# A two-layer trunk on one core: two norm rows carried through a DRAM row, and five turns of compressed weights moved next to the value products

## The chip, the cores and the metric

The kernel runs on one core of one Trainium2 chip. The metric is the device time of one execution in microseconds (us). The core has five engines that each work through an instruction list of their own: PE (TensorE, the matrix engine), DVE (VectorE), ACT (ScalarE), POOL (GpSimd) and SP (SyncE, which here only issues transfers). They wait for each other on semaphores. Transfers are issued by an engine onto a DMA queue and done by 16 DMA engines.

## What is computed

A sequence of 512 positions of width 1024 goes through two layers. Layer 0 mixes by gated linear attention, layer 1 by a sparse attention with a compressed, a selected and a windowed branch, whose keys and values come from a shared projection of the input of layer 1. Both layers also attend to a memory of 256 rows, and both end in a gated convolutional FFN. Cut to what the change touches:

```python
def rmsnorm(x, g):
    y = x * lax.rsqrt(jnp.mean(x * x, axis=-1, keepdims=True) + EPS)
    return y * g

mem_kv = rmsnorm(mem, norm_mem[i]) @ w_mem_kv[i]             # both layers: 256 rows, 1024 -> 512
kv = (rmsnorm(h, kv_norm) @ w_kv).reshape(B, S, 6, G, Dh)    # layer 1: 512 rows
kc, vc = compress(kv[0], 0), compress(kv[1], 1)              # 31 blocks of 32 positions, stride 16
...
s_c = einsum('bgrqd,bgkd->bgrqk', qb, kc) + common_bias(d_c)   # 12 heads x 512 queries x 31 blocks
p_c = masked_softmax(s_c, d_c >= 0)
o_c = einsum('bgrqk,bgkd->bgrqd', p_c, vc)
o = gb[..., 0:1] * o_c + gb[..., 1:2] * o_s + gb[..., 2:3] * o_w
```

All is float32.

## The kernel before

Activations lie transposed: a tile `h[k]` holds 128 of the 1024 features on its partitions and the 512 positions along the free axis. A float32 product is made of three faster ones: each operand is split into a rounded part and the rest (`xh`, `xl` for activations, `wh`, `wl` for weights, written by ACT and DVE at L287/L288 or L304/L305), and PE adds `xh*wh + xh*wl + xl*wh`. A projection onto 128 outputs (`projA`, L326) is 24 such matmuls, called steps 0 to 23, into one bank of PSUM. PSUM's banks come in four names, `acc`, `sc`, `pt` and `po`, with two banks each, and a bank is used again when its readers have finished. The weights come through SP's queue into `wraw`.

A normalised projection needs one factor for each position. The squares are summed over the feature tiles into `sqacc`, and `rms_sums` sums over the partitions by eight narrow matmuls (L368); DVE scales (`rc`, L378) and POOL takes the power -1/2 (L379). `rc` then holds position 128t+p at partition p, column t. Where the outputs stand on partitions and the positions along the free axis, the factor is wanted as a row, the same on all partitions (`rb`). `rms_rows` makes it on PE: it transposes each column of `rc`, broadcast to 128 columns, into `pt` (L386), and ACT copies the bank out (L390).

Each engine's order is fixed when the kernel is built: a scheduler lists the instructions as the program issues them, by estimated ready times, and `behind` adds order where the author wants it. The `at` argument of `projA` runs code at a given step of a projection.

Three places matter.

- First memory (`mem_kv` with l = 0, at about 40 to 60 us): `rms_sums` at step 12 of the first key projection; `rms_rows` after the sixth group of three products of the value projection; then the keys are scaled by the row (`mkf`, DVE), split (`mK`, ACT L412 and DVE), and the values scaled by `rcm` (`mV`, ACT). The same function runs again for layer 1.
- Second mixer (`nsa_layer`, at about 580 to 603 us): four projections `kvc` (j = 0, 1 and m = 0, 1) into the two banks of `acc`. In the second one the sums come at step 0 and the rows at step 12 (`rms_at`). Each result is then scaled by the row (`kf`, DVE L1576), which frees its bank, and stored four times into `T` by SP's queue. The third projection takes the bank of the first.
- Sparse attention (`nsa_layer`, at about 700 to 822 us): twelve steps s; a pair of heads a has an even step (query tiles 0 and 3) and an odd one (1 and 2), and each step goes through places i = 0 to 5. A step computes the scores of step s+1 (`sc`, `po` from `K` and `Qh`, `Ql`), softmax weights on DVE, ACT and POOL, brings them by DMA into `R`, turns them on PE (`pt<-ident,R`, L1718, and the copies into `PT`, L1913), runs at i = 4 the value products of step s-1 (`po<-PT,V`: 20 matmuls of 64 columns, of which the profile makes 40; `values`), and fills in matmuls of other projections (L1717 with `xh`, `wh`, and L1003 in the last steps). The compressed branch is the generator `compressed(a)` in three pieces: products with the compressed keys and the exponentials; the sums and the scaling of `Pc` on POOL (L1825, L1826); and the turn: four transposes `pt<-ident,Pc` of 64 columns on PE, a copy to `PcT` by ACT (L1831) and a subtraction by DVE (L1832). For a pair a+1 the first piece runs at i = 4 of an odd step, the second at i = 0 of the next, even step, and the third at i = 0 of the odd step after it. `PcT` is first read at i = 4 of that odd step, by `values`.

## Time and profile before

| | |
|---|---|
| time, median of 3 runs | 1223.89 us (1223.47 to 1224.72) |
| the profiled execution's own time | 1224.9 us |
| its span | 1223.1 us, granted TensorE clock 0.998 |
| PE, weight loads | 1211.6 us (99%), 1077.9 us (88%) |
| DVE, ACT, POOL | 912.5 us (75%), 729.7 us (60%), 275.2 us (23%) |
| DMA queues, share of 16 engines | hardware 34.0%, POOL's 10.7% |

The profile is one execution. Busy times are the sums over an engine's instructions, with overlapping matmuls not counted twice; the span is from the first instruction to the last. The time lies 1.8 us above the span. In the groups of instructions the three numbers after a colon are the least, the median and the longest duration in ns. Durations of matmuls include the time in the pipeline, so that one starts before the one ahead has ended; what a matmul costs is read from the distance of the starts.

### The profile page before, as it was taken

The page shows a single profiled execution, that of the slowest core. Times are in us where ns is not written, and L with a number is a line of the kernel's source. Part 1 is how long each engine was busy: PE and PEld are TensorE (multiplying, and loading weights), DVE is VectorE, ACT ScalarE, POOL GpSimd, SP SyncE. Part 2 cuts the span into 40 slices and gives each one's busy share as a digit, 9 for nine tenths or more (in the row PEclk, how much of TensorE's full clock was granted, in tenths as well). Part 3 has the DMA queues.
Part 4 walks back from the last instruction along what each step waited for, and adds up shares of the span by engine and source line. Part 5 has one row for each costly group of instructions (what it writes and reads, how often), then busy time and mean ns, then how long its engine had stood idle before and what let it go on. Part 6 is the DMA issues. An engine that isn't in the chain of part 4 may idle for free.

```text
span 1223.1 us, 22059 instructions
## 1 busy us (share of the span) xinstructions
PE 1211.6 (99%) x8321; PEld 1077.9 (88%) x8321; DVE 912.5 (75%) x1637; ACT 729.7 (60%) x1459; POOL 275.2 (23%) x290
## 2 busy tenths in 40 slices
PE   9999999999999999999999999999999999999997
PEld 8887889889999998888888878878899999998887
DVE  7667886698888889644776878875788888889431
ACT  7656655467666667333544677764576666675331
POOL 1000000014444420000003366660034444400000
PEclk9999999999999999999999999999999999999999
DMA  7541113236666652323725467643256666633221
GB/s 262 155 138 60 36 36 104 103 101 171 158 157 156 156 128 86 125 87 109 210 104 172 125 207 234 206 166 121 72 144 163 157 156 156 156 104 108 103 69 69
DMA packets 59776, 163.09 MB, mean 133 GB/s; under 512 B 7309, under 2 KB 13384, under 8 KB 59670
## 3 DMA queue, kind: packets, MB, share of 16 engines
q1 hardware_dynamic: 47638, 140.66, 34.0%
q0 software_dynamic: 10944, 19.93, 10.7%
q8 instruction: 65, 1.06, 0.4%
q10 hardware_dynamic: 1088, 1.10, 0.3%
q14 instruction: 41, 0.34, 0.1%
HBM read 116.13 MB, written 2.15 MB: 97 GB/s over the span
## 4 chain that ended last, share of the span: by engine, by line
PE 94%; DVE 2%; issue 1%; ACT 1%; DMA 1%; POOL 1%; POOLq 0%; DVEq 0%; ACTq 0%
PE pt L1186 18%; PE acc L326 10%; PE po L1186 9%; PE acc L1419 7%; PE acc L1003 6%; PE po L1358 5%; PE sc L1358 5%; PE sc L1186 5%; PE po L346 3%; PE acc L789 3%; PE po L1717 3%; PE acc L1717 2%; PE acc L1482 2%; PE acc L1623 2%; PE acc L346 2%; PE sc L1717 1%
## 5 line engine op out<-in xcount | busy, mean ns | idle before, releaser
L287 ACT ACTIVATE wh<-wraw 128x1024 fp32r<-128x1024 f32 (+1 forms) x105 | 109.4, 1043 | 140.6 <-PE sc L1358 29.6
L288 DVE TENSOR_TENSOR wl<-wraw,wh 128x1024 fp32r<-128x1024 f32 (+1 forms) x105 | 128.7, 1227 | 74.8 <-ACT wh L287 74.0
L1175 DVE TENSOR_TENSOR wl<-wraw,wh 128x1024 fp32r<-128x1024 f32 x76 | 72.6, 955 | 7.0 <-ACT wh L1172 7.0
L326 PE MATMUL acc<-xh,wh 128*128 128x512 f32 x184 | 72.6, 395 | 0.0
L326 PE MATMUL acc<-xl,wh 128*128 128x512 f32 x184 | 71.9, 391 | 0.0
L326 PE MATMUL acc<-xh,wl 128*128 128x512 f32 x184 | 71.9, 391 | 0.0
L1419 PE MATMUL acc<-a,wh 128*128 128x512 f32 x228 | 71.1, 389 | 0.0
L1166 POOL DMA_DIRECT2D wraw<-rbw x38 | 33.4, 879 | 153.3 <-DVE wl L1175 113.9
L1175 DVE TENSOR_TENSOR wl<-rbw,wh 128x1024 fp32r<-128x1024 f32 x38 | 46.5, 1225 | 26.5 <-ACT wh L1172 26.5
L1056 DVE SCALAR_TENSOR_TENSOR hc<-acc,ntap,hc 128x511 f32<-128x511 f32 x76 | 56.9, 749 | 10.0 <-ACT hc L1053 8.0
L1172 ACT ACTIVATE wh<-wraw 128x1024 fp32r<-128x1024 f32 x76 | 63.9, 843 | 0.6 <-DMA wraw<-rbw 0.5
L1797 POOL TENSOR_TENSOR P<-P,ssm 128x256 f32<-128x256 f32 (+3 forms) x48 | 61.8, 1309 | 1.9
L1056 DVE SCALAR_TENSOR_TENSOR hc<-acc,vec,hc 128x511 f32<-128x511 f32 x76 | 56.9, 749 | 3.0 <-ACT hc L1053 1.7
L1789 ACT ACTIVATE P<-P,smn 128x128 f32<-128x128 f32 (+3 forms) x96 | 53.3, 558 | 7.5 <-DVE smn L1787 6.9
L1161 POOL TENSOR_TENSOR rbw<-s,rbw 128x512 f32<-128x512 f32 x36 | 47.8, 1329 | 36.8 <-DVE xh L1064 19.0
L1358 PE MATMUL po<-a,wh 128*128 128x512 f32 x144 | 56.0, 389 | 0.0
L1358 PE MATMUL sc<-a,wh 128*128 128x512 f32 x144 | 56.0, 389 | 0.0
L1172 ACT ACTIVATE wh<-rbw 128x1024 fp32r<-128x1024 f32 x38 | 40.2, 1059 | 23.4 <-issue 20.5
L1419 PEld LDWEIGHTS acc<-a,wh 128*128 128x128 f32 x228 | 42.8, 188 | 8.9
L1155 POOL TENSOR_TENSOR s<-wraw,rbw 128x512 f32<-128x512 f32 x34 | 44.8, 1317 | 21.4 <-DVE wl L1175 21.4
L1172 ACT ACTIVATE wh<-s 128x512 fp32r<-128x512 f32 x38 | 24.0, 632 | 42.1 <-PE pt L1186 42.1
L1419 PE MATMUL acc<-a,wl 128*128 128x512 f32 x114 | 44.3, 389 | 0.0
(726 smaller groups left out, 4338.7 us busy)
## 6 DMA issues: line engine op xcount, KB each, us to landing
wraw<-in_wp SPq DMA_DIRECT2D x156, 512.0 KB, 3.2
rbw<-in_wp SPq DMA_DIRECT2D x38, 512.0 KB, 4.4
rbw<-rbw POOLq DMA_DIRECT2D x38, 256.0 KB, 4.2
wraw<-rbw POOLq DMA_DIRECT2D x38, 256.0 KB, 3.3
R<-P SPq DMA_DIRECT2D x12, 512.0 KB, 3.3
strip<-vecd SPq DMA_DIRECT2D x12, 448.0 KB, 5.6
R<-P SPq DMA_DIRECT2D x11, 384.0 KB, 3.3
qd<-qf SPq DMA_DIRECT2D x24, 128.0 KB, 3.2
```

Source lines behind the costliest of these rows:

```text
L287: self.made = nc.scalar.activation(wh, raw, AF.Copy)
L288: self.left = nc.vector.tensor_tensor(out=wl, in0=raw, in1=wh.bitcast(F32), op=ALU.subtract)
L326: self.last = self.nc.tensor.matmul(ps[:M, :N], u[:, M * k:M * k + M], x[k][i][:, :N], start=n == 0, stop=n == 23)
L1003: self.nc.tensor.matmul(ps[:, cols], a[:, o], b[:, cols], start=start and i == 0 and k == ks[0], stop=stop and k == 5 and i == 2)
L1056: return [nc.vector.scalar_tensor_tensor(out=c[:, 2 - i:], in0=u[:, :S - 2 + i], scalar=tap(half, j, i, neg), in1=c[:, 2 - i:], op0=ALU.mu ...
L1172: return after("A", nc.scalar.activation(out, x, AF.Copy))
L1175: return after("D", nc.vector.tensor_tensor(out=out, in0=x, in1=hi.bitcast(F32), op=ALU.subtract))
L1186: after("P", nc.tensor.matmul(bank[:, :256], w[:, o], x, start=start and k + i == 0, stop=k == 3 and i == 2, skip_group_check=True))
L1358: after("P", nc.tensor.matmul(first[m], a[:, o], x, start=r + i == 0, stop=r == NJ - 1 and i == 2))
L1419: nc.tensor.matmul(ps, a[:, o], x, start=n == 0, stop=n == 3 * NJ - 1)
L1717: mm = lambda *args, **kw: pe(nc.tensor.matmul(*args, **kw))
L1797: nc.gpsimd.tensor_tensor(out=P, in0=P, in1=f[:, i, :].unsqueeze(2).to_broadcast([128, 2, 128 * t + 128]), op=ALU.mult)
```

## The change

The change has three parts.

First memory and second mixer: a new function `rms_carried` stands in for `rms_sums` and `rms_rows`. After the sums it writes `rc` by a DMA of POOL's queue into a row in DRAM, each partition's two or four numbers side by side (8 or 16 bytes), reads that row back to all 128 partitions by a second DMA of the same queue, and lets ACT copy it to `rb` with the positions put back into order. PE takes no part after the sums. In the first memory the sums stay where they were; in the second mixer they move from step 0 of the second projection to step 14 of the first. The second memory keeps `rms_rows`.

Sparse attention: the third piece of `compressed` runs at i = 4 of the even step, right behind the value products of the step before, and no longer at i = 0 of the odd step. This concerns five turns (even steps 2, 4, 6, 8 and 10); the one at step 0 stays at i = 0.

```diff
-    def rms_at(self, first, second, N=S, tag=""):
-        return {first: lambda: self.rms_sums(N, tag), second: lambda: self.rms_rows(N, tag, self.last)}
+    def rms_carried(self, N, tag):
+
+        nc, nt = self.nc, N // 128
+        self.rms_sums(N, tag)
+        row = self.t(self.dram, [1, N], "row" + tag, bufs=2)
+        nc.gpsimd.dma_start(row.rearrange("o (p t) -> p (o t)", t=nt), self.rc)
+        rows = self.t(self.tmp if not tag else self.mpool, [128, N], "sq" + tag, bufs=2)
+        nc.gpsimd.dma_start(rows, row.to_broadcast([128, N]))
+        self.rb = self.t(self.tmp if not tag else self.mpool, [128, N], "rb" + tag, bufs=1)
+        self.spread = nc.scalar.copy(self.rb.rearrange("q (t p) -> q t p", t=nt), rows.rearrange("q (p t) -> q t p", t=nt))
...
-            self.projA(pk[0], self.wget(self.W[f"memk{l}"][0]), N=MEM, x=mx, at={12: lambda: self.rms_sums(MEM, "m")})
+            self.projA(pk[0], self.wget(self.W[f"memk{l}"][0]), N=MEM, x=mx, at={12: lambda: (self.rms_sums if l else self.rms_carried)(MEM, "m")})
...
-            self.rms_rows(MEM, "m", self.last)
+            if l:
+                self.rms_rows(MEM, "m", self.last)
...
-                        self.projA(pk[m], self.wget(self.W["kvc"][2 * j + m], GKV), at=self.rms_at(0, 12) if m and not j else ())
+                        self.projA(pk[m], self.wget(self.W["kvc"][2 * j + m], GKV), at={14: lambda: self.rms_carried(S, "")} if m + j == 0 else ())
...
                         if i == 4:
                             run(before)
+                            if s and not qts[0]:
+                                run(c)
...
-                        if i == 0:
+                        if i == 0 and not qts[0]:
                             run(c)
```

What this does to the engines' lists, at the places that the prediction speaks of. Numbers behind a name are the buffers; brackets name the engine or DMA queue that is waited for (DMASW is POOL's queue). In the new kernel the line numbers after `rms_carried` are 8 to 11 higher.

PE in the second mixer before, around the seam of the first and second projection:

```order
L326 MATMUL acc_6462<-xh_6431,wl_6466 128x512 [waits DVE_49]
L326 MATMUL acc_6462<-xl_6432,wh_6465 128x512 [waits DVE_49]
L368 MATMUL pt_6528<-ones_112,sqacc_6039 64x1 [waits PE_49]
L368 MATMUL pt_6528<-ones_112,sqacc_6039 64x1 x7
L326 MATMUL acc_6507<-xh_6041,wh_6510 128x512
```

Its step 12, with the four transposes:

```order
L326 MATMUL acc_6507<-xl_6066,wh_6510 128x512
L386 MATMUL pt_6552<-ident_107,rc_6537 128x128 [waits PE_49,Pool_49]
L386 MATMUL pt_6552<-ident_107,rc_6537 128x128 x3
L326 MATMUL acc_6507<-xh_6158,wh_6510 128x512
L326 MATMUL acc_6507<-xh_6158,wl_6511 128x512
```

PE in the new kernel, at step 14 of the first projection; the second and third follow with nothing between their matmuls:

```order
L326 MATMUL acc_6463<-xh_6159,wh_6466 128x512 [waits Activation_49]
L326 MATMUL acc_6463<-xh_6159,wl_6467 128x512 [waits DVE_49]
L368 MATMUL pt_6498<-ones_112,sqacc_6040 64x1 [waits DVE_49,PE_49]
L368 MATMUL pt_6498<-ones_112,sqacc_6040 64x1 x7
L326 MATMUL acc_6463<-xl_6160,wh_6466 128x512
```

The sums stand ten matmuls earlier, and the L386 rows are gone.

POOL at the same place in the new kernel, with the two transfers behind the power; before, the two L379 rows stood next to each other:

```order
L379 TENSOR_TENSOR rc_6507<-rc_6507,mhalf_126 128x4 [waits DVE_49]
L397 DMA row_6510<-rc_6507 128x4 [waits Pool_49]
L399 DMA sq_6512<-row_6510 128x512 [waits DMASW0_49,Activation_49]
L379 TENSOR_TENSOR rcm_7132<-rcm_7132,mhalf_126 128x2 [waits DVE_49]
L286 TENSOR_TENSOR wraw_7270<-wraw_7270,vec_82 128x1024 [waits DMAHW3_49,DMAHW4_49,DMAHW1_49,DMAHW6_49,DMAHW0_49,DMAHW7_49,DMASW5_49,Activation_49]
```

ACT's copy stands at the same place of its list in both kernels; it now waits for POOL's queue where it waited for PE, and the splits of the second memory (`mh`, `sqm`) are behind it:

```order
L357 ACTIVATE sqm_7073<-mt_7071 128x256 [waits DMAHW0_49,DVE_49]
L401 COPY rb_6514<-sq_6512 128x512 [waits DMASW1_49]
L304 ACTIVATE mh_1251_7076<-mt_7071,vec_82 128x256
L357 ACTIVATE sqm_7082<-mt_7080 128x256 [waits DMAHW1_49,DVE_49]
L304 ACTIVATE mh_1255_7085<-mt_7080,vec_82 128x256
```

PE in the sparse attention before, where a turn stands (odd step 3, place 0), between matmuls of a projection and score products:

```order
L1717 MATMUL acc_8170<-xh_6158,wl_8166 128x512
L1718 MATMUL pt_8307<-ident_107,Pc_8096 64x128 [waits Activation_49,Pool_49]
L1718 MATMUL pt_8307<-ident_107,Pc_8096 64x128 x3
L1717 MATMUL sc_8319<-K_1146_6445,Qh_1514_8250 128x512 [waits DVE_49]
L1717 MATMUL sc_8319<-K_1146_6445,Ql_1515_8251 128x512
```

The same turn in the new kernel (even step 2, place 4), behind the last of the 20 value products:

```order
L1726 MATMUL po_8064<-PT_8126,V_6450 64x128
L1727 MATMUL pt_8250<-ident_107,Pc_8096 64x128 [waits Activation_49,Pool_49]
L1727 MATMUL pt_8250<-ident_107,Pc_8096 64x128 x3
L1726 MATMUL sc_8264<-K_1149_6448,Qh_1465_8008 128x384 [waits DVE_49]
L1726 MATMUL sc_8264<-K_1149_6448,Ql_1466_8009 128x384
```

The turn moved ahead by 18 rows of PE's list; its ACT copy and DVE subtraction moved with it. On DVE at step 8 the subtraction now stands ahead of the split `Ql` and of the copy that frees the next bank of `pt`:

```order
L302 TENSOR_TENSOR xl_9152<-po_8982,xh_9151 128x512 [waits Activation_49]
L1841 TENSOR_TENSOR PcT_1423_7863<-pt_9155,PcT_1423_7863 64x512 [waits Activation_49]
L302 TENSOR_TENSOR Ql_1717_9163<-qd_9058,Qh_1716_9162 128x512 [waits DMAHW1_49,DMAHW0_49,Activation_49]
L1922 COPY PT_9107<-pt_9174 128x512 [waits PE_49]
L1796 ISA P_9116,smn_9168<-po_9180,strip_8873 128x384 [waits PE_49]
```

Before, that copy and `Ql` came first and the subtraction stood thirteen rows behind `Ql`. At step 10 the order is the same in kind: ACT's `PcT` ahead of the copies out of `pt`, DVE's subtraction ahead of the copy of the next bank.

## The prediction, made before the changed kernel had run

> **What bounds the kernel now.** I read the page's busy shares first, then the chain that ended last, then the timeline of each engine at the three places that the diff touches.
>
> ```profile
> PE 1211.6 (99%) x8321; PEld 1077.9 (88%) x8321; DVE 912.5 (75%) x1637; ACT 729.7 (60%) x1459; POOL 275.2 (23%) x290
> ```
>
> ```profile
> PE 94%; DVE 2%; issue 1%; ACT 1%; DMA 1%; POOL 1%; POOLq 0%; DVEq 0%; ACTq 0%
> ```
>
> The matrix engine (PE) is busy for 99% of the span and is 94% of the chain. A microsecond is won where PE gets less to do or waits less, and lost where PE is made to wait. Work on DVE, ACT, POOL and the DMA queues costs nothing until PE asks for its result. So I price every edit as PE time, and then ask whether the new, longer route delivers in time. In the timeline rows the columns are start, busy us, engine, line, operation; the bracket is idle time before it and what ended it.
>
> **Removed: six transposes on PE.** Matmuls overlap, so the price is how far the transposes push the next start, not their duration.
>
> ```profile
> 52.71 0.28 PE L346 MATMUL po<-wh,ml 128*128 128x256 f32 x1
> 52.83 0.38 PE L386 MATMUL pt<-ident,rcm 128*128 128x128 f32 x2
> ...
> 53.17 0.28 PE L346 MATMUL po<-wl,mh 128*128 128x256 f32 x1
> ...
> 579.71 0.39 PE L326 MATMUL acc<-xh,wh 128*128 128x512 f32 x1
> ...
> 582.89 0.39 PE L326 MATMUL acc<-xl,wh 128*128 128x512 f32 x1
> ...
> 585.24 0.63 PE L368 MATMUL pt<-ones,sqacc 128*64 128x1 f32 x16
> ...
> 588.44 0.39 PE L326 MATMUL acc<-xl,wh 128*128 128x512 f32 x1
> 588.67 0.60 PE L386 MATMUL pt<-ident,rc 128*128 128x128 f32 x4
> ...
> 589.33 0.39 PE L326 MATMUL acc<-xh,wl 128*128 128x512 f32 x1
> ...
> 591.85 0.39 PE L326 MATMUL acc<-xh,wh 128*128 128x512 f32 x1
> ```
>
> Mixer: from step 0 to step 14 (579.71 to 582.89) a 512-wide product takes 3.18/14 = 0.227 us, so a 256-wide one 0.114. Memory: from 52.71 to 53.17 are 0.46 us with two 256-wide products; 0.46 - 0.23 = 0.23, say **0.22 us** for two transposes, half of what four cost the mixer. There, from 588.44 to 589.33 are 0.89 us with two; 0.89 - 0.45 = **0.43 us** for four transposes. The column sums (585.24) only move to step 14 and cost the same there.
>
> **Added for the mixer: a round trip of two DMAs.** The rows that price it:
>
> ```profile
> 586.05 0.15 DVE L378 TENSOR_SCALAR rc<-pt 128x4 f32<-128x4 f32 x1
> ...
> 589.92 0.69 DVE L1576 TENSOR_TENSOR kf<-acc,rb 128x512 f32<-128x512 f32 x1
> ...
> 597.49 0.69 DVE L1576 TENSOR_TENSOR kf<-acc,rb 128x512 f32<-128x512 f32 x1 [1.52 <-PE acc L326]
> ...
> 586.28 1.21 POOL L379 TENSOR_TENSOR rc<-rc,mhalf 128x4 f32<-128x4 f32 x1 [6.67 <-DVE rc L378]
> ...
> 589.30 0.59 ACT L390 COPY rb<-pt 128x512 f32<-128x512 f32 x1
> ```
>
> ```profile
> rbw<-rbw POOLq DMA_DIRECT2D x38, 256.0 KB, 4.2
> wraw<-rbw POOLq DMA_DIRECT2D x38, 256.0 KB, 3.3
> ...
> wgl<-in_wgl SPq DMA_DIRECT2D x1, 144.0 KB, 2.3
> ...
> cmask<-in_c_cmask ACTq DMA_DIRECT2D x1, 16.0 KB, 2.5
> ```
>
> The last column is us from issue to landing. Sums at 582.89; DVE's rc came 0.81 after the sums' start (585.24 to 586.05), so now near 583.7, and since three splits are queued ahead of it on DVE I take 584.0. POOL's power takes 1.21: 584.2 to 585.4. Write of 512 numbers: no row shows so small a transfer from POOL's queue. By size the nearest is 2.5, by queue 3.3, the least is 2.3; I take 2.5, since 3.3 has 256 KB in it. POOL then waits for it, and issues the 256 KB read: bounds 2.3 (144 KB) and 4.2, taken 3.0, near POOL's own 3.3 but without reading from SBUF. Rows land at 585.45 + 2.5 + 0.1 + 3.0 = **591.05** (590.15 to 593.05).
>
> Who waits: ACT's copy, then DVE's first kf. From the copy's start to kf's end were 1.31 us (589.30 to 590.61); with 0.1 for the wake, kf ends at landing + 1.4 = 592.45. kf releases a bank of acc that the third projection needs. That one began at 591.85, and without the transposes PE is there at 591.4. **Stall 592.45 - 591.4 = 1.05 us**, bounds 0.15 and 3.05; net of the transposes **+0.6** (-0.3 to +2.6; -0.43 if the trip were free). Behind the waiting copy on ACT and the waiting kf on DVE, and behind kf's stores on SP's queue, stand splits and loads for later projections; the row at 597.49 is their cover: the third kf waited 1.52 us for PE, so lateness up to there is swallowed.
>
> By the Trainium skill's "DMA: Bandwidth & Descriptors", section "Anatomy of one DMA — SWDGE (gpsimd) path", a DMA takes 2.0 us plus bytes over 436 kB per us; as an estimate from that page the trip is 2.0 + 2.6, the rows land at 590.15 and the net is about -0.3. The section adds that the fixed part is mostly the receipt of the write and long when the target is HBM, which speaks against the change; no run here shows a write this small.
>
> **Added for the first memory: the same trip under load.**
>
> ```profile
> 48.05 1.74 POOL L379 TENSOR_TENSOR rcm<-rcm,mhalf 128x2 f32<-128x2 f32 x1 [19.75 <-DVE rcm L378]
> ...
> 53.25 0.37 ACT L390 COPY rbm<-pt 128x256 f32<-128x256 f32 x1 [1.32 <-PE pt L386]
> 54.11 1.74 ACT L412 ACTIVATE mK<-mkf 64x256 fp32r<-64x256 f32 x4 [0.49 <-DVE mkf L481]
> 56.53 0.84 ACT L490 ACTIVATE mV<-po,rcm 128x256 f32<-128x256 f32 x2 [0.69 <-PE po L346]
> 59.40 1.06 ACT L287 ACTIVATE wh<-wraw 128x1024 fp32r<-128x1024 f32 x1 [2.02 <-DMA wraw<-in_wp]
> ...
> 60.49 2.54 DVE L288 TENSOR_TENSOR wl<-wraw,wh 128x1024 fp32r<-128x1024 f32 x2 [4.16 <-ACT wh L287]
> ...
> 62.33 0.39 PE L326 MATMUL acc<-xh,wl 128*128 128x512 f32 x1
> ```
>
> POOL ends at 49.79. The engines are full of loads, so I take 2.5 + 0.1 + 3.3: rows at 55.75 (bounds 2.3 + 2.3 and 3.3 + 4.2: 54.5 to 57.4). From the copy to the end of mV are 3.55 us, so ACT reaches wh at 59.3; before it sat idle 2.02 us until 59.40, and PE meets the wl at 62.33 with half a us to spare. So it is free up to a landing at 56.35, and one for one after that. **-0.22** (to +0.85).
>
> **Moved: five turns of compressed weights.** One turn is four 64-column transposes, an ACT copy and a DVE subtraction.
>
> ```profile
> 736.78 0.40 PE L1717 MATMUL acc<-xh,wl 128*128 128x512 f32 x1
> 737.02 0.60 PE L1718 MATMUL pt<-ident,Pc 128*64 128x128 f32 x4
> ...
> 737.69 0.39 PE L1717 MATMUL sc<-K,Ql 128*128 128x512 f32 x1
> ...
> 754.25 0.45 PE L1717 MATMUL sc<-K,Qh 128*128 128x384 f32 x1
> 754.53 0.34 PE L1717 MATMUL sc<-K,Ql 128*128 128x384 f32 x1
> ...
> 757.49 0.52 PE L1718 MATMUL pt<-ident,R 128*128 128x128 f32 x4 [0.56 <-DMA R<-P]
> ...
> 795.13 0.44 PE L1717 MATMUL sc<-K,Qh 128*128 128x384 f32 x1
> ...
> 799.38 0.39 PE L1717 MATMUL sc<-K,Ql 128*128 128x256 f32 x1 [0.75 <-DVE Ql L302]
> ...
> 815.79 0.44 PE L1717 MATMUL sc<-K,Qh 128*128 128x384 f32 x1
> ...
> 818.06 0.54 PE L1718 MATMUL pt<-ident,R 128*128 128x128 f32 x4 [0.81 <-ACT PT L1913]
> ...
> 753.42 0.62 POOL L1826 TENSOR_TENSOR Pc<-Pc,cf 128x256 f32<-128x256 f32 x1
> ...
> 795.46 0.61 POOL L1826 TENSOR_TENSOR Pc<-Pc,cf 128x256 f32<-128x256 f32 x1
> ```
>
> A turn costs 737.69 - 736.78 - 0.45 = 0.46 us where it stands, hardly more than the mixer's four full-width transposes (0.43), so the change of width costs it almost nothing. After the value products (they end just before 754.25, 795.13 and 815.79) a K product of 384 columns holds the next start up by 0.28 us (754.25 to 754.53); at 0.227 for 512 columns it should be 0.17. At least 0.11 is lost there, perhaps as much again before it; the turn, with the same 64 columns, may take that loss's place. I take 0.2 a turn, bounds 0 and 0.26.
>
> The Trainium skill's "TensorEngine Tiling (Array Packing)", section "Key Properties", says a change of tiling mode drains the engine. As an estimate by that page two drains per turn would go, 0.16 each (0.39 of duration less 0.23 of pitch), 1.6 us in all, which in place of my 0.2 a turn would lower the sum by 0.6; the 0.03 between 0.46 and 0.43 disagrees.
>
> Then readiness, turn by turn. At steps 2, 4 and 6 POOL ends Pc about 0.2 us before the value products end (754.04 against 754.25): no wait, -0.2 each; at step 4 PE in any case waits 0.56 at 757.49, which swallows what the turn adds ahead of it, so -0.4. At step 8 POOL ends Pc at 796.07 but PE is there at 795.13: a new wait of 0.95. The turn itself adds 0.25 ahead of Ql, and the wait of 0.75 at 799.38 goes in exchange, as does the turn's 0.46 behind it: **+0.35** allowing for Ql now queued behind the turn's ACT copy and DVE subtraction. At step 10 Pc is ready, but the two banks of pt are now freed by the turn's DVE subtraction and by a copy queued behind it: walking ACT and DVE in their new order from 815.79 gives PE waits of about 0.7, 0.6 and 0.25 where one of 0.81 stood, **+0.6** with the turn's saving. Sum -0.2 - 0.4 - 0.2 + 0.35 + 0.6 = **+0.15** (-1.0 if steps 8 and 10 go like the others, -2 if they also lose the old waits; +1.4).
>
> **Sum.** -0.22 + 0.6 + 0.15 = +0.5 on the profiled execution's 1224.9 us. That stands 1.0 above the median of 1223.89; the change is the same for both, so the forecast is **1224.4 us**. A difference under 0.2%, 2.45 us here, can't be told from no change.
>
> **Rivals.**
> (1) The rows come late at the mixer. For it: DRAM must confirm the write before the read is sent, and both share engines with loads. Slower by 2.45 overall needs a stall of 2.95, so a landing from about 593 on; at 594, +3.5, 1227.4. Against: 593.05 is the sum of the longest rows. 0.12.
> (2) The rows come late at the first memory: every DMA engine is full there, so two trips could take 9 us. Landing at 59 is a stall of 2.65, +3.2 in all, 1227.1. It decides from 58.3. Against: the longest rows end at 57.4. 0.06.
> (3) The turns pay fully and the old waits at 757.49, 799.38 and 818.06 take up what remains; -2.0 there, -0.22 and -0.43: 1221.2, faster. Against: POOL's 796.07. That end 0.07; partly so (1221.5 to 1223.2, same) 0.17.
> (4) Nothing happens: trips hidden, turns free of gain and loss: -0.65, 1223.2; part of the same.
>
> **Numbers.** Likeliest, from 1223.2 to 1225.5: 0.50. Turns paying partly 0.17 and a mixer landing of 592 to 593 (1225.5 to 1226.3) 0.08 are within 0.2% too: same 0.75. Slower 0.12 + 0.06 = 0.18; faster 0.07. The range leaves out a tenth at each end: 1222.2, between (3) and its partial case, to 1227.0, into (1).
>
> **What would show it.** The two L386 groups gone from these places; the row read landing near 591 and PE idle about 1 us at L326, released by DVE's kf; no new idle on PE near 62; the Pc transposes behind the value products, with no wait at steps 2 to 6, one of 1 us on POOL at step 8, and several short ones on DVE and ACT at step 10. The prediction is wrong if the trip takes over 7.6 us, if PE waits near 62, or if a K product behind a turn starts as late as it does behind value products.

## The result, and the profile after

The changed kernel took 1240.54 us (median of 4 runs, 1240.09 to 1241.81), the kernel before 1223.81 (4 runs, 1223.47 to 1224.72): a ratio of 1.0136, interval 1.0124 to 1.0148. The forecast was 1224.4, its range ended at 1227.0, and slower had a chance of 0.18: wrong by 16 us.

The page of the changed kernel, busy shares and chain:

```profile
PE 1214.9 (98%) x8315; PEld 1080.3 (87%) x8315; DVE 910.9 (74%) x1637; ACT 731.7 (59%) x1459; POOL 277.5 (22%) x294
...
PE 89%; DMA 3%; ACT 3%; DVE 2%; issue 2%; POOL 1%; SPq 0%; POOLq 0%; DVEq 0%; ACTq 0%
```

PE does six matmuls less and is busy for 3.3 us more; DMA and ACT now hold 3% of the chain each. Where PE waits (total, times, longest), in the changed kernel:

```profile
PE acc L326 <- ACT wh L287: 6.9, 1, 6.9
PE acc L326 <- DVE kf L1585: 4.1, 1, 4.1
...
PE pt L1727 <- POOL Pc L1835: 0.9, 1, 0.9
...
PE sc L1726 <- DVE Ql L302: 0.6, 1, 0.6
PE pt L1727 <- DVE PcT L1841: 0.6, 1, 0.6
...
PE pt L1727 <- ACT PT L1922: 0.5, 1, 0.5
```

The first two lines are new, and each is one single wait. To see what each place costs in all, I set every matmul's start against the start of the same matmul before, and call the difference the shift. It is -0.8 us at 50 us (start-up) and -1.0 behind the place of the two saved transposes, goes to +9.0 in the first memory (+10.0), to +14.45 in the second mixer (+5.55), and to +15.54 in the sparse attention (+1.2, with small losses on the way); after that it stays. The spans differ by 15.8 us, so these three places are the whole change.

First memory, timeline of the changed kernel (POOL, ACT, PE), and the two transfers with their time from issue to landing:

```profile
49.32 0.77 POOL L397 DMA_DIRECT2D rowm<-rcm  x1 [0.31 <-POOL rcm L379]
57.06 0.57 POOL L399 DMA_DIRECT2D sqm<-rowm  x1 [6.96 <-DMA rowm<-rcm]
...
63.66 0.42 ACT L401 COPY rbm<-sqm 128x256 f32<-128x256 f32 x1 [12.51 <-DMA sqm<-rowm]
...
67.05 2.94 ACT L287 ACTIVATE wh<-wraw 128x1024 fp32r<-128x1024 f32 x3
...
68.16 0.79 PE L326 MATMUL acc<-xh,wh 128*128 128x512 f32 x1 [6.88 <-ACT wh L287]
```

```profile
sqm<-rowm POOLq DMA_DIRECT2D x1, 128.0 KB, 6.6
rowm<-rcm POOLq DMA_DIRECT2D x1, 1.0 KB, 7.2
```

The trip from the first issue to ACT's copy took 14.3 us (49.32 to 63.66: 7.2 for the write, 0.5 until the read is issued, 6.6 for the read) where I had 5.9. The weight split `wh`, which stands on ACT behind the copy and the keys, starts at 67.05 instead of 59.40.

Second mixer, the same views of the changed kernel:

```profile
594.34 0.64 POOL L397 DMA_DIRECT2D row<-rc  x1 [0.30 <-POOL rc L379]
598.27 0.55 POOL L399 DMA_DIRECT2D sq<-row  x1 [3.28 <-ACT sqm L357]
...
602.70 1.09 ACT L401 COPY rb<-sq 128x512 f32<-128x512 f32 x1 [4.49 <-DMA sq<-row]
...
603.82 0.69 DVE L1585 TENSOR_TENSOR kf<-acc,rb 128x512 f32<-128x512 f32 x1 [5.06 <-ACT rb L401]
...
604.57 0.50 PE L326 MATMUL acc<-xh,wh 128*128 128x512 f32 x1 [4.11 <-DVE kf L1585]
```

```profile
sq<-row POOLq DMA_DIRECT2D x1, 256.0 KB, 4.4
...
row<-rc POOLq DMA_DIRECT2D x1, 2.0 KB, 3.4
```

The stretches of 4 us behind the two waits in the changed kernel; after the busy times stand the granted clock, the DMA share and GB/s:

```profile
64.00:68.00 4.00, 0.00 (x0) 0.00 (x0) 2.44 (x6) 3.41 (x8) 0.00 (x0) 0.80 0.00 0
68.00:72.00 4.00, 3.38 (x7) 2.39 (x8) 3.86 (x4) 2.78 (x5) 0.00 (x0) 0.50 0.37 132
72.00:76.00 4.00, 4.00 (x16) 3.19 (x16) 2.89 (x5) 1.73 (x3) 0.00 (x0) 0.84 0.72 244
...
604.00:608.00 4.00, 3.43 (x10) 2.74 (x11) 4.00 (x12) 4.00 (x14) 0.00 (x0) 0.72 0.54 120
608.00:612.00 4.00, 4.00 (x17) 3.25 (x16) 1.84 (x8) 0.66 (x2) 0.00 (x0) 0.86 0.91 236
```

In the kernel before, the clock is 1.00 in all stretches from 60 to 76. Here PE comes back from its wait at half clock: the wait is followed by a second loss that no list of waits shows.

### The profile page after: what moved, and what is told of

Same layout as the page of the kernel before. It is cut to its first block, busy times and chain, and to the rows that moved or that the text cites. A ratio compares the mean times of both kernels' runs of the same rounds, so it can differ in the third digit from the quotient of the medians.

```text
span 1238.9 us, 22058 instructions
## 1 busy us (share of the span) xinstructions
PE 1214.9 (98%) x8315; PEld 1080.3 (87%) x8315; DVE 910.9 (74%) x1637; ACT 731.7 (59%) x1459; POOL 277.5 (22%) x294
## 4 chain that ended last, share of the span: by engine, by line
PE 89%; DMA 3%; ACT 3%; DVE 2%; issue 2%; POOL 1%; SPq 0%; POOLq 0%; DVEq 0%; ACTq 0%
PE pt L1195 17%; PE po L1195 9%; PE acc L326 9%; PE acc L1428 7%; PE acc L1012 6%; PE po L1367 5%; PE sc L1367 5%; PE sc L1195 5%; PE po L1726 3%; PE acc L1726 3%; PE acc L798 3%; PE po L346 2%; PE acc L1491 2%; PE acc L1632 2%; PE acc L346 2%
## 5 line engine op out<-in xcount | busy, mean ns | idle before, releaser
L326 PEld LDWEIGHTS acc<-xh,wh 128*128 128x128 f32 x184 | 35.5, 193 | 19.0 <-ACT wh L287 7.3
```

The lines of the kernel that those rows point to most:

```text
L326: self.last = self.nc.tensor.matmul(ps[:M, :N], u[:, M * k:M * k + M], x[k][i][:, :N], start=n == 0, stop=n == 23)
```

## The experiments

In each expectation, A and B are the theories stated there; a shift is always that of PE's starts against the kernel before. Ratios are to the kernel before, timed on the same chip.

### One part of the change at a time

Only the first memory (the other two parts as before):

```diff
-    at={14: lambda: self.rms_carried(S, "")} if m + j == 0 else ()
+    at=self.rms_at(0, 12) if m and not j else ()
...
-    if s and not qts[0]:
-        run(c)
...
-    if i == 0 and not qts[0]:
+    if i == 0:
```

> Only the first memory's rows carried through DRAM; mixer and turns as before. Theory A (the three parts add up, and the first memory is the largest): the shift of PE's starts between 60 and 80 us was +10.0 us less the 0.2 of two transposes, so about 1233.6 us, with a wait of about 6.9 us at L326 near 61 us. Rival B (the waits of one part come from what another part moved): more than 1 us away from that. Rival C (the trip is free alone): 1223.6 us.

1235.54 us, ratio 1.0089 (1.0075 to 1.0103). Landings 6.9 and 6.5 us, PE's wait 6.6 + 0.5, shift +9.1. The median lies 1.9 us above A's 1233.6 (the profiled execution, 1233.27, is the lowest of the four), so that by the letter it is B; but the long wait and the shift are there without the other two parts. The loss is of the memory's own making.

Only the second mixer (the memory with `rms_sums` and `rms_rows`, the turns as before):

> Only the second mixer's rows carried. Theory A: the shift around 600 us was +5.55 us, so about 1229.4 us, with a wait of about 4.1 us at L326 on kf and a lower granted clock for some us behind it. Rival B (with the memory undisturbed its loads fall differently and the trip is short, as I forecast: a stall of 1.05): about 1224.4 us.

1229.97 us, 1.005 (1.0034 to 1.0066). Landings 3.4 and 4.6, `kf` waited for 4.3 us; the shift goes from -1.4 to +5.4, by 6.8. Timeline of PE in this kernel, the seam and the end of the slow stretch:

```profile
589.77 0.39 PE L326 MATMUL acc<-xl,wh 128*128 128x512 f32 x1
594.47 0.80 PE L326 MATMUL acc<-xh,wh 128*128 128x512 f32 x1 [4.32 <-DVE kf L1584]
595.06 0.63 PE L326 MATMUL acc<-xh,wl 128*128 128x512 f32 x1
595.49 0.63 PE L326 MATMUL acc<-xl,wh 128*128 128x512 f32 x1
...
600.15 0.39 PE L326 MATMUL acc<-xh,wl 128*128 128x512 f32 x1
```

The thirteen distances from 594.47 to 600.15 make 5.68 us where 13 x 0.227 would be 2.95: the start-to-start distance is 0.43 (595.06 to 595.49) instead of 0.23, which it is again from 600.15 on. So 4.3 us of wait and 2.7 us of slow clock, less the transposes, are the 6.8.

Only the turns, and only those of steps 2, 4 and 6 (`a < 4` in the condition):

> Only the five turns moved. Theory A: the shift between 700 and 840 us was +1.2 us, so about 1225.0 us: about 0 at steps 2 and 6, -0.7 at step 4, +0.1 to +0.3 at step 8, +2 at step 10 and behind it. Rival B (the turns lose only because the earlier parts moved the stage): 1223.0 us or less.

> Only the turns of steps 2, 4 and 6 moved; those of steps 8 and 10 stay where they were. Theory A (the losses are those of steps 8 and 10): about -0.8 us, 1223.0 us, and no wait on POOL's Pc or DVE's PcT. Rival B (what steps 8 and 10 show follows from the earlier turns having moved): 1224 us or more.

All five: 1225.25 us, 1.0008 (0.9999 to 1.0016); shift in the stage from -0.12 at 700 us to +0.55 at 840, +0.7. Steps 2, 4 and 6: 1223.86 us, 0.9993 (0.9985 to 1.0002); -0.79 to -1.42, so -0.6. PE's waits in the stage with all five turns moved:

```profile
PE pt L1729 <- POOL Pc L1837: 0.9, 1, 0.9
...
PE pt L1729 <- DVE PcT L1843: 0.6, 1, 0.6
PE pt L1729 <- ACT PT L1924: 0.5, 1, 0.5
```

With three turns neither `Pc` nor `PcT` is in the list. The last two turns turn a small gain into a small loss. The turn of step 10 in its new place, with all five moved, and the two K products behind it:

```profile
814.27 0.63 PE L1729 MATMUL pt<-ident,Pc 128*64 128x128 f32 x4
814.65 0.42 PE L1728 MATMUL sc<-K,Qh 128*128 128x384 f32 x1
814.91 0.34 PE L1728 MATMUL sc<-K,Ql 128*128 128x384 f32 x1
```

The first K product holds the next start up by 0.26 us, where it was 0.28 behind the value products alone. The K product starts 0.59 us behind the start of the last value product instead of 0.20. So it is at all five turns, but for the added wait at step 8. A turn thus costs 0.37 us here (0.39 - 0.02), against the 0.46 of its old place.

Only the turn of step 10:

```diff
-    if s and not qts[0]:
+    if s == 10:
         run(c)
...
-    if i == 0 and not qts[0]:
+    if i == 0 and s != 11:
         run(c)
```

> Only the turn of step 10 moved. Theory A (the two banks of pt, freed late by the turn's DVE subtraction and by copies behind it, make PE wait at step 10, and the idle lowers the clock): the shift behind 840 us is +1.5 to +2.5, waits on DVE PcT and ACT PT as with all five moved, time about 1226.3 us. Rival B (step 10 loses only after an earlier step 8 has reordered the stage): shift under +0.5.

1226.38 us, 1.0013 (1.0004 to 1.0022); shift 0.45 to 0.90 across the stage, +0.5, with waits of 0.5 (`PcT`), 0.5 (`PT`) and 0.2. The rest arises after the stage, most of it near 910 us; the trace of the three turns alone gathers 1.1 us there too, so it is not this turn's. With all five turns moved the same step costs more: the shift goes from -1.5 at 812 us to +0.55 at 832, and in the changed kernel from +13.45 to +15.55, about 2 each. There the granted clock falls behind the waits, to 0.80 and 0.77 between 832 and 840 in the changed kernel; with the turn alone it stays at 1.00. The same stretch with the five turns alone:

```profile
816.00:820.00 4.00, 2.65 (x14) 1.97 (x15) 3.62 (x9) 2.58 (x7) 0.75 (x2) 0.85 0.43 164
820.00:824.00 4.00, 4.00 (x46) 3.35 (x46) 0.69 (x1) 0.48 (x1) 2.58 (x3) 0.73 0.02 4
```

### Why the memory's trip takes 14 us

All of these start from the memory-only kernel, but for the two probes beside the kernel before, which say so. The loads of `lad` (4 x 384 KB) moved behind two weight loads:

```diff
-    nc.sync.dma_start(lad[...], la[...])
+    self.behind(nc.sync.dma_start(lad[...], la[...]), self.loaded)
...
-    spread(0)
```

> The memory rows carried alone; the four transfers of 384 KB from la to lad, issued before at 45 to 51 us, stand behind two weight loads, so that the DMA engines have less to do while the row is written. Theory A (the trip is long because its packets and its receipts stand in line with the loads): write in under 4.5 us in place of 6.9, the wait at L326 under 4 us in place of 6.6, time below 1231 us. Rival B (a write of 8-byte pieces into DRAM takes that long by itself): write still over 6 us, wait over 6 us.

1234.21 us, 1.0079 (1.0063 to 1.0094). The write got faster (6.9 to 5.7), the read slower (6.5 to 9.4), and PE waited 7.5 + 0.5 us. The write was hardly freed of load, since the weight loads went out in the place of `lad` (share 0.93 and 0.82 from 50 to 54); the four loads then ran beside the read.

Both transfers on ACT's hardware queue in place of POOL's:

```diff
+    (nc.scalar if tag else nc.gpsimd).dma_start(row..., self.rc)
```

> The memory rows carried alone, both DMAs issued by ACT onto a hardware queue in place of POOL's software queue. Theory A (load on the engines sets the trip): still over 10 us in all, PE's wait within 2 us of 6.6. Rival B (POOL's queue sets it: 3.5 us until the first packet of either DMA): trip under 8 us, wait under 2 us, time about 1226 us.

1233.36 us, 1.0073 (1.0058 to 1.0088). The write took 5.7, the read at most 7.5 (issued at 55.40, copied out at 62.91), and PE waited 4.2 + 1.5 us. The trip is about as long as on POOL's queue; the kind of queue is not the cause.

The same two transfers at quieter places, beside the kernel before's own work (in the first layer at 127 to 144 us, with nobody on PE waiting):

> The kernel before, with four round trips that nobody waits for in the quiet stretch of 92 to 183 us (DMA engines about a tenth busy): 16-byte pieces on POOL's queue, 8-byte pieces on POOL's queue, 16-byte pieces on SP's queue, 4-byte pieces on SP's queue, each read back to 128 partitions. Theory A (load makes the trip long): POOL's write 2.5 to 3 us and its read 2.5 to 3.5, whatever the piece. Rival B (the kind of transfer makes it long): POOL's write over 3.4 us and its read over 4 even here.

One run, 1224.5 us. First a write of 2 KB in 16-byte pieces at a DMA share of 0.01 and its read, alone on the engines (the 0.33 of its stretch is its own 256 KB), then 1 KB in 8-byte pieces at 0.56 and its read at 0.28:

```profile
probe<-mhalf POOLq DMA_DIRECT2D x1, 2.0 KB, 2.5
...
sq<-probe POOLq DMA_DIRECT2D x1, 256.0 KB, 3.6
...
probe<-mhalf POOLq DMA_DIRECT2D x1, 1.0 KB, 4.7
...
sq<-probe POOLq DMA_DIRECT2D x1, 128.0 KB, 4.0
```

The quiet trip is near what I had forecast (2.5 and 3.0 to 3.3). The probes on SP's queue left no landing in the trace and say nothing.

The four loads of `lad` left out (zeros from POOL; the decays are not computed):

> p_memory (only the first memory's norm row is carried) without the four loads of lad, 384 KB each, which ran during the trip; lad is set to zero by POOL early instead, so the decays are left out of the computation. The weight loads stay. Theory A (the DMA engines' load makes the trip long): the share in the windows of the trip falls from 0.99 and 1.31 to 0.6 or less, the write lands after 3 to 4.7 us instead of 6.9, the read after 4 to 5 instead of 6.5; rows near 58.5 instead of 64, PE waits 1 to 3 us near L326 instead of 7, shift +2 to +5, time 1226 to 1229. Theory B (a write of 256 numbers in pieces of 8 bytes and its read cost 13 us at this place whatever else runs): landings, wait and shift as in p_memory, +9, 1235.

1229.97 us, 1.004 (1.0024 to 1.0055); shift +6.2. Neither theory alone:

```profile
sqm<-rowm POOLq DMA_DIRECT2D x1, 128.0 KB, 3.7
rowm<-rcm POOLq DMA_DIRECT2D x1, 1.0 KB, 7.1
```

The read, at a share of 0.60 from 58 to 60 and 0.06 behind it, is down from 6.5 to 3.7: that is load. The write still took 7.1. It was little relieved, for without `lad` the weight loads go out earlier (from 49.44 instead of 51.74), and the share from 50 to 54 is 0.76 and 0.90, against 0.99 and 1.03. In the packets, around its landing, sixteen 4 KB packets of the weight load behind it last 3.0 to 3.8 us each; the median of such packets is 0.16. The memory-only kernel and the changed one have 14 and 15 of them over 1.5 us there; the kernel before has none at this place, and the kernel with the loads of `lad` moved has none either.

The piece doubled to 16 bytes, each factor written twice:

```diff
-    self.rc = self.t(self.small, [128, nt], "rc" + tag, bufs=2)
+    wide = self.t(self.small, [128, 2 * nt], "rc" + tag, bufs=2)
...
+    nc.gpsimd.dma_start(row.rearrange("o (p t) -> p (o t)", t=2 * nt), wide)
```

> p_memory with each of the 256 factors written twice, so that a partition's piece is 16 bytes instead of 8 (2 KB in all, as in the mixer); the read then brings 256 KB instead of 128 KB, and ACT picks every other pair. The loads beside it are the same. Theory A (the load of the DMA engines makes the write late): landing 6 to 7.5 us after the issue as in p_memory (6.9), the read 6.5 to 8, PE waits 6 to 8 us, shift +9 to +10.5, time 1235. Theory B (pieces of 8 bytes are what DRAM is slow with): landing 3.4 to 4.7, none of the weight load's packets over 1.5 us, PE's wait 3 us shorter than p_memory's, shift +5 to +6.5, time 1231.

1233.3 us, 1.0069 (1.0053 to 1.0086).

```profile
sqmw<-rowm POOLq DMA_DIRECT2D x1, 256.0 KB, 6.8
rowm<-rcm POOLq DMA_DIRECT2D x1, 2.0 KB, 4.8
```

4.8 us where 8-byte pieces took 6.9 under the same load, and none of the long packets: B for the write. 4.8 is still 2.3 above the quiet 2.5. The shift, +8.8, is only 0.3 below the memory-only kernel's, and B's +5 to +6.5 did not come: PE waited 5.0 + 0.5 us, 1.6 less, but then ran at clock 0.50 from 68 to 72 and 0.80 from 72 to 76, where the memory-only kernel has 0.50 and 0.95.

A write from SBUF to SBUF at this place, in 8-byte pieces, added to the kernel before, beside the unchanged way through PE:

```diff
+    there = self.t(self.mpool, [128, nt], "row" + tag, bufs=1)
+    nc.gpsimd.dma_start(there, self.rc)
+    nc.gpsimd.tensor_copy(self.t(self.mpool, [128, nt], "seen", bufs=1), there)
```

> The kernel before, with one DMA of POOL's queue added in the first memory right behind the power, as in p_memory, but from SBUF to SBUF: 128 partitions with 8 bytes each, which a copy on POOL waits for. Nothing else waits for it; the norm rows are made by PE as before. Theory A (load): 6 to 7 us from issue to landing, as into DRAM at this place. Theory B (the target in DRAM is what is slow): 2 to 3.5 us, and no packet of the loads over 1.5 us. Time as before by both, 1224 to 1225.

1225.72 us, 1.0014 (1.0004 to 1.0024).

```profile
rowm<-rcm POOLq DMA_DIRECT2D x1, 1.0 KB, 5.2
```

5.2 us without touching DRAM, between the two theories, and no long packets at this place. So a target in DRAM is not needed to make the write slow; the load is enough (2.5 to about 5), and 8-byte pieces into DRAM add some 2 more.

The write's own packets in the traces show where each of the two acts. I split the time at the end of the last packet that carries data: from the issue to there, and from there to the landing.

| write | to the last packet, us | from there to the landing, us |
|---|---|---|
| quiet probe, 16-byte pieces into DRAM | 1.5 | 1.0 |
| mixer, 16-byte pieces into DRAM (changed kernel, mixer-only kernel) | 2.4, 2.9 | 1.0, 0.5 |
| memory, 16-byte pieces into DRAM | 3.7 | 1.1 |
| memory, SBUF to SBUF, 8-byte pieces | 4.2 | 1.0 |
| memory, 8-byte pieces into DRAM (memory-only, changed, without `lad`, `lad` moved) | 4.1, 4.1, 3.8, 4.0 | 2.8, 3.1, 3.3, 1.7 |
| probe at 0.56, 8-byte pieces into DRAM | 2.9 | 1.9 |
| mixer, 4-byte pieces into DRAM (the plain copy, below) | 3.1 | 6.0 |

The load stretches the first part, small pieces into DRAM the second. Without `lad` the first part is shorter by 0.3 only, so that run could not show what load does to the write.

### What PE's wait costs beside itself

29 idle matmuls (result not used) in the memory's wait:

```diff
+    idle = self.ps("pt")
+    for _ in range(29):
+        ins = nc.tensor.matmul(idle, self.x[0][0][:, :128], self.x[0][0], start=True, stop=True)
+        self.behind(ins, self.last)
+        self.last = ins
```

> The memory rows carried alone, as in the run of that part, and 29 matmuls of 512 columns of no use put into PE's wait (29 x 0.227 = 6.6 us). Theory A (idle PE is paid twice: the wait, and a lower granted clock for some us behind it): the wait is filled, the granted clock stays 1.00 between 64 and 76 us, and the shift behind 80 us falls from +9.1 to about +6.8 us. Rival B (the 2.5 us beyond the wait come from the late weights, not from the clock): the shift stays at +9.1, with new waits on wl or wh behind the filler.

1235.22 us, 1.0092 (1.0075 to 1.0109): no gain. The clock stays at 1.00 in all four stretches from 60 to 76, but in this run the trip took longer (landings 7.8 and 6.9), PE still waited 1.3 + 0.8, and the shift was +9.2. It doesn't decide. The mixer's trip repeats better, so the same was tried there, with 20 matmuls:

> p_mixer (only the mixer's norm row is carried) with 20 idle matmuls of 128x512 on PE between the second and the third projection, 20 x 0.227 = 4.5 us where PE waited 4.3 us for kf. The matmuls' result is not used. In p_mixer the thirteen starts after the wait stood 5.68 us apart in all instead of 13 x 0.227 = 2.95, at a granted clock of 0.66 and 0.50 in two windows. Theory A (the wait itself lowers the granted clock, and this costs 2.7 us on top of the wait): the third projection begins at about the same time, at 0.227 from start to start and at clock 1.00; PE's shift against before falls from 6.8 to 4.1 to 4.5, the time by about 2.5, to 1227.5. Theory B (the clock is lowered by something else at this place, as the burst of stores and loads that starts at the same time): the slow starts stay, or come with the idle matmuls, and the shift stays at 6.8 to 7, the time at 1230.

1230.49 us, 1.0049 (1.0036 to 1.0061). Clock and busy time where the mixer-only kernel has its slow stretch, first that kernel, then the filled one:

```profile
592.00:596.00 4.00, 1.53 (x4) 1.25 (x5) 2.27 (x5) 3.39 (x8) 0.00 (x0) 0.66 0.11 24
596.00:600.00 4.00, 4.00 (x11) 3.17 (x10) 3.71 (x13) 2.57 (x9) 0.00 (x0) 0.50 0.90 204
```

```profile
592.00:596.00 4.00, 4.00 (x19) 3.15 (x18) 0.89 (x2) 2.02 (x4) 0.00 (x0) 1.00 0.33 129
596.00:600.00 4.00, 4.00 (x19) 3.31 (x19) 4.00 (x13) 3.95 (x13) 0.00 (x0) 1.00 0.69 156
```

PE does 19 starts from 596 to 600 instead of 11, and the shift behind the seam is 4.2 instead of 6.8: the slow clock was caused by the idle time, and cost 2.6 us there. This half of A holds. But the time didn't fall, since a new wait came 12 us later:

```profile
PE acc L1612 <- DVE kf L1590: 1.6, 1, 1.6
```

```profile
604.09 3.75 DVE L1664 TENSOR_TENSOR tp<-T,vec 128x1024 f32<-128x1024 f32 x2 [3.00 <-DMA T<-kf]
607.73 0.70 DVE L1590 TENSOR_TENSOR kf<-acc,rb 128x512 f32<-128x512 f32 x1
```

DVE had been held up by the row as well (5.3 us at the first `kf`), so the stores into `T` are late, and `tp` waits for them. The filler also changed DVE's order: here `tp` stands ahead of the third `kf`, for which PE waits; in the mixer-only kernel it stands behind it. So the lateness and the new order make this wait together, and what the filler would gain in the old order no run shows. The wait gives back 1.8 of the 2.6 us. This trace, of the longest of the five executions (1232.47), gathers more later on; the trace with the SBUF write, whose mixer is that of before, gathers 1.5 us between 650 and 700 as well, so that this is not shown to come from the row.

### Can the mixer's wait be stepped round?

The third and fourth projection in the banks of `sc`, so that they need no `kf` first:

```diff
-    pk.append(self.ps("acc"))
+    pk.append(self.ps("sc" if j else "acc"))
```

> Only the second mixer's rows carried, and the third and fourth projection write the two banks of sc in place of the two of acc, so that PE no longer needs the first kf to go on. Theory A (the bank held by the late kf is the whole of that part's loss): no wait at L326 on kf, granted clock 1.00 throughout, -0.4 us against before from the four transposes, where the part alone had +5.5. Rival B (the late rows are met again a little later, in the splits behind the waiting copy and kf, or in T's stores): new waits of 2 us or more between 592 and 615 us, time above 1226 us.

1230.11 us, 1.0046 (1.0031 to 1.0062). The wait for `kf` is gone. DVE in this kernel, and PE's one wait:

```profile
600.89 0.69 DVE L1584 TENSOR_TENSOR kf<-sc,rb 128x512 f32<-128x512 f32 x1 [0.32 <-DMA T<-kf]
603.03 3.77 DVE L1658 TENSOR_TENSOR tp<-T,vec 128x1024 f32<-128x1024 f32 x2 [1.46 <-DMA T<-kf]
...
609.47 0.68 DVE L1608 TENSOR_TENSOR gt<-acc,rb 100x512 f32<-100x512 f32 x1
```

```profile
PE pt L368 <- DVE gt L1608: 3.4, 1, 3.4
```

B: `kf` is late, its stores into `T` are late, `tp` waits for them on DVE, and `gt` behind it keeps PE waiting at 610. Behind the wait the granted clock is 0.62 and 0.52 from 608 to 616, and the shift goes from -0.6 to +5.4. The loss is the same, some 16 us further on.

Plain copy, with the row written in 4-byte pieces in order instead of 16-byte pieces to be sorted afterwards:

```diff
-    nc.gpsimd.dma_start(row.rearrange("o (p t) -> p (o t)", t=nt), self.rc)
+    nc.gpsimd.dma_start(row.rearrange("o (t p) -> p (o t)", p=128), self.rc)
```

> Only the second mixer's rows carried, written in 4-byte pieces in the order of the positions, so that the read lands as the row itself and ACT's copy is a plain one. Theory A (the copy's 1.09 us come from its reading with a step of 16 bytes): copy 0.6 us, the wait on kf 0.5 shorter than 4.3 if the write of 512 pieces takes no longer. Rival B (more and smaller pieces cost more on the queue than the copy saves): write more than 0.5 us longer than 3.4, wait 4.3 or more.

1236.95 us, 1.01 (1.0086 to 1.0114). ACT's copy took 0.62 us instead of 1.09, so sorting costs 0.5; but the write took 9.1 instead of 3.4, PE waited 9.6.

The banks of `sc` and the turns of steps 2, 4 and 6, the parts that had looked best:

> The version that the runs point to: memory as before, mixer's rows carried with the third and fourth projection in the banks of sc, turns of steps 2, 4 and 6 moved, those of 8 and 10 not. Theory A: -0.4 from the mixer and -0.4 to -0.8 from the turns, about 1 us below before, at the edge of what can be told. Rival B: no gain, because the waits at Ql and PT in steps 8 and 10 take the turns' gain back.

1230.48 us, 1.004 (1.0028 to 1.0053). No version tried is faster than the kernel before; the three turns alone are the same as it.

## Why the prediction was wrong, point by point

**What bounds the kernel.** Right: PE's waits decide, and the shift at three places is the whole change.

**The term for the first memory (-0.22, to +0.85) is the main failure: measured +10.0, or +9.8 with the saved transposes.** The step that failed is "I take 2.5 + 0.1 + 3.3: rows at 55.75 (bounds ... 54.5 to 57.4)". The trip was priced from medians over transfers at other places, although the same paragraph says that the engines are full there. Measured: 2.5 and 3.6 with nothing beside them; in the memory 6.9 to 7.8 for the write, at a share around 1, and 6.5 to 6.9 for the read, at 0.95 from 58 to 60 and 0.44 behind it in the changed kernel. Between the landing and the next issue lie 0.5 us, not 0.1. "The longest rows" were no bound: medians of a whole kernel bound nothing at its most loaded place. The load alone makes the write 4.8 to 5.2 (16-byte pieces; SBUF target); the 8-byte pieces add some 2. Behind the landing the path is the one written (`wh`, then `wl`, released last), with a little more to spare: the changed kernel runs 0.8 us ahead here, so its copy at 63.66 stands 63.66 + 0.8 - 56.35 = 8.1 us behind the end of what I had called free, and PE's waits were 6.88 + 0.47 = 7.35.

**The term for the mixer (+0.6, to +2.6): measured +5.55.** The write was issued where I had it (594.34, less the shift of 8.9). Write 3.4 for 2.5, 0.5 for 0.1 until the read's issue, read 4.4 for 3.0, and the copy 1.09 for 0.59: I had taken the duration of the old copy for one that reads in another order. The wait of 1.05 became 4.11. Rival (1) is what happened, with the place and the mechanism that it names, and its chance of 0.12 was too low for the same reason. The cover that I gave for later lateness ("swallowed up to the third kf", 1.52 us) is real but small against this.

**A term was missing: the clock after a wait.** In neither the sum nor a rival does PE run slower after idling. The windows show 0.50 behind the memory's wait and, in the mixer-only kernel, behind the mixer's (0.72 and 0.86 there in the changed kernel), and the filled kernel shows that the idle time is the cause: 2.6 us at the mixer in the mixer-only kernel. In the memory, +10.0, counted from behind the saved transposes, less waits of 7.35 leaves some 2.6 for it. The Trainium skill's "TensorE: Matmul & The Clock Gate", section "What's actually happening", states it: idle for about 3.4 us, the array falls to half its clock until it has been busy for as long again. The 0.43 us from start to start agree with the 426.7 ns that its section "Wait — 56ns, not 53.3ns?" gives for 512 columns at half clock. A wait of 1.05 us, as forecast, is shorter than that window, so by this rule the term would have been nil; the measured waits of 4.1 and 6.9 are past it. In the traces half clock behind a wait lasts 3.41 us or two or three times that, which agrees (3.41 at the mixer of the changed kernel, 6.83 in its memory).

Where it begins no run here settles: behind PE's waits of 3.2 us and more it always came, behind waits of 1.3 + 0.8 and of 1.6 it did not, but with all five turns moved the clock also fell at step 10, where no wait is above 0.6 us, and the Trainium skill's rule does not cover that.

**The turns (+0.15, -1.0 to +1.4): measured +0.7 alone, +1.2 with the rest.** Steps 2, 4 and 6: -0.8 forecast, -0.6 measured. Step 8: a wait of 0.95 on POOL's `Pc` forecast, 0.9 measured. Step 10: +0.6 forecast, +0.5 measured alone, with the waits on `PcT`, `PT` and one more, as forecast (0.7, 0.6 and 0.25 against 0.5, 0.5 and 0.2). The waits were right and the sum lies in its bounds, but in part by luck. The 0.2 a turn was the gain of a loss that the turn would stand in for; that loss stays (0.26 for 0.28), and the place is worth some 0.1 a turn (0.46 - 0.37). Where the rest of the gain of steps 2, 4 and 6 comes from the runs do not show. With all five turns steps 2 to 8 gave 0.7 to 1.2 where I had 0.45, and step 10 cost about 2, since the clock fell behind its waits.

**The rivals.** (1) and (2) both came true, in places that I had priced as independent at 0.12 and 0.06. They are not independent: one misjudged number, the trip under load, decides both. (3) fell to step 8 and 10.

**The estimate that I weighed.** By the Trainium skill's "DMA: Bandwidth & Descriptors", section "Anatomy of one DMA — SWDGE (gpsimd) path", the trip in the mixer would take 2.0 + 2.6; measured 3.4 + 4.4, so the estimate from its formula was worse than the rows. The Trainium skill's section "Latency and other measured facts" there says that access to HBM takes 0.2 us on average and 2 at high load, and the section that I cited puts most of the fixed part into the receipt (the confirmation that the data have landed); that load makes it longer agrees, and I treated it as an aside. The split does not agree: the quiet write spent 1.5 of its 2.5 us ahead of the end of its last packet, and under load the part behind it stayed near 1 us, into DRAM in 16-byte pieces as into SBUF.

**What stays open.** Why in the memory long packets of the loads come with 8-byte pieces into DRAM (not in the probe at a share of 0.56, where the write took 4.7, nor with `lad` moved, where it took 5.7), and which of the two holds up the other, was not settled. Nor was how wait and slow clock divide in the memory, since the one filled run there had a longer trip.

## What to carry to other kernels

A route through DRAM is priced at the load of the place where it runs: read the DMA share of that stretch, and take transfers of that stretch, not medians of the whole kernel; two dependent transfers in the loaded stretch cost 12 to 15 us here, not 6. A stall of 3.2 us or more on the matrix engine cost its length and then 2 to 3 us more at half clock here, and lateness that another bank or a filler hid came back at a later consumer in both trials: before replacing work on the busiest engine by a route, ask whether all that hangs on the route, not only its first reader, has slack for it. Here transposes priced at 0.65 us were exchanged for 15.

## What the hardware showed that I had not expected

- The size of pieces of a tiny write into DRAM: 512 numbers took 3.4 us in 16-byte pieces and 9.1 in 4-byte pieces at the same place; 256 numbers took 6.9 in 8-byte pieces and, written twice in 16-byte pieces with double the bytes, 4.8.
- Around the landing of a write of 1 KB in 8-byte pieces, 14 to 16 packets of 4 KB of another queue lasted 1.6 to 3.8 us instead of 0.16.
- Load acts on such a write ahead of its last packet (1.5 us quiet, about 4 in the memory), pieces of 4 or 8 bytes into DRAM behind it (1.7 to 6.0 us, against 0.5 to 1.1).
- A hardware queue (5.7 and 7.5 us) and POOL's queue (6.9 and 6.5) are about equally slow under that load.
- 20 idle matmuls (4.5 us) in the place of a wait of 4.3 us kept the granted clock at 1.00; the time stayed, as another wait came.
